# Seven Strassen products of a GeGLU up projection in another order: the product with the four-quarter weight sum moves from fourth to sixth place

## The chip, the cores and the metric

The kernel runs on 1 core of one Trainium2 chip. The metric is device time in microseconds (us) of one execution; each kernel's number is the median of several runs. The kernel before took 1378.93 us in the median of 3 runs (1378.06 to 1379.33).

## The reference, cut to what matters

The model is a two-layer encoder (512 tokens, width 1024, float32). Each layer ends in a GeGLU channel mixer, and the change lies in its up projection `hn @ w_up`, which has 2 x 2816 output columns: a gate half and a value half.

```python
def conv_geglu_ffn(hn, w_up, conv_w, conv_b, w_down):
    u = depthwise_conv_centered(hn @ w_up, conv_w, conv_b)
    gate, val = jnp.split(u, 2, axis=-1)
    return (jax.nn.gelu(gate, approximate=True) * val) @ w_down
...
for layer in range(DEPTH):
    ...
    f = conv_geglu_ffn(rms_norm(x, norm_ffn_pre[layer]), ffn_w_up[layer], ffn_conv_w[layer],
                       ffn_conv_b[layer], ffn_w_down[layer])
    x = x + rms_norm(f, norm_ffn_post[layer])
```

## The kernel before, in words

**Three-term products.** Every float32 factor is held as a high half and a low half (`hi + lo`). `split` (L104 on) makes them: a cast on ScalarE (L107) writes the high half, a subtraction on VectorE (L108) writes the low half. One product is then three matmuls (`mm3`): high by high (L116), low activation by high weight or its mirror (L117), and the third pairing (L118). In the up projection the weights are the stationary operand, so L116 and L118 need the high half of the weight (`whi`) and L117 needs its low half (`wlo`).

**The up projection.** The 22 column blocks `f` (128 gate and 128 value columns each) are walked in `ffn` (L500 on). Blocks 0 to 5, 12, 13, 20 and 21 are done plainly: two projections (gate and value) of 24 matmuls each, 512 tokens wide. The pairs that start at f = 6, 8, 10, 14, 16, 18 (`UP`, L391) go through `up_strassen`: seven products instead of eight, each of 24 matmuls 256 tokens wide, into PSUM tiles `mm` (banks `a`) and `pu` (banks `b` and `d`). So three Strassen pairs stand in a row, then two plain blocks, then three pairs, then two plain blocks, then the down projection. Both layers do the same.

**What one pair needs.** Four weight quarters of 128 x 1024 are loaded through SyncE's DMA queue: `q[11]` into a tile `wu`, `q[12]` and `q[22]` into `wst` (3 buffers, shared with all other weight loads), `q[21]` into `gain` (2 buffers). Seven weight blocks are multiplied: q11, q12+q22, q11+q12+q22, q11+q12+q21+q22, q11+q12, q21 and q22 in this order. The four additions are on VectorE (L451), 128 x 1024 each. Each block is split into one of 4 `whi` and one of 4 `wlo` buffers, so a split has to wait until the product four places earlier has read its buffers.

**What comes out.** Results are copied by ScalarE or added by VectorE into `G` and `V` (L487 to L495). Then `tail` does the convolution, the gelu and the gating product for the pair's two column blocks: per block 2 activations for the convolution (L511) and one gelu (L518) on ScalarE, 4 convolution steps (L512, L513) and one product into `H` (L520) on VectorE. In between, `E.chore` issues copies and accumulating copies of the down weights from GpSimd's queue (L274), each tied to a finished product.

**What sets the order.** The code is written with tiles; a scheduler puts the instructions of each engine into one fixed order by readiness and priority, and every engine then works its list strictly in that order. The weight preparation stands under a raised priority (L455), but only the order that the scheduler found counts at run time: an addition or a split can stand behind convolution steps that were ready earlier.

Of the kernel before, what the change touches and what calls it, by code (L numbers as in the profile page):

```python
# [8 lines left out]
F32 = mybir.dt.float32  # L9
# [8 lines left out]
P = 128  # L18
S = 512
NT = S // P  # L20
D = 1024
# [411 lines left out]
def up_strassen(E, pool, w_up, f, X, G, V):  # L433

    nc, tc = E.nc, E.tc
    low, high = slice(0, HW), slice(HW, S)

    def load(pool, name, s, h, tag=None):  # L440
        st = pool.tile([P, 1024], F32, name=name, tag=tag or name)
        nc.sync.dma_start(st.rearrange("p (f c) -> p f c", f=2),
                          w_up[s, f:f + 2, :, h * 512:h * 512 + 512].rearrange("f p c -> p f c"))
        return st

    def parts(st):
        hi, lo = E.whi.tile([P, 1024], R32, name="whi"), E.wlo.tile([P, 1024], R32, name="wlo")
        E.split(hi, lo, st)
        return hi, lo

    add = lambda o, x, y: nc.vector.tensor_tensor(o, x, y, op=ALU.add)  # L451
    q = {}

    def weights(i):
        with tc.high_priority(60):  # L455
            if i == 0:
                q[11] = load(pool, "wu", 0, 0, f"e{UP.index(f) % 2}")
                return parts(q[11])
            if i == 1:
                q[12], q[22] = load(E.wst, "wst", 1, 0), load(E.wst, "wst", 1, 1)  # L460
                add(q[11], q[11], q[12])
                add(q[12], q[12], q[22])
                return parts(q[12])
            if i == 2:
                q[0] = E.gain.tile([P, D], F32, name="gain")
                add(q[0], q[11], q[22])
                return parts(q[0])
            if i == 3:
                q[21] = load(E.gain, "gain", 0, 1)
                add(q[0], q[0], q[21])  # L470
                return parts(q[0])
            return parts(q[{4: 11, 5: 21, 6: 22}[i]])

    a = [E.mm.tile([P, S], F32, name="mm") for _ in range(2)]
    b, d = ([E.px.tile([P, S], F32, name="pu", tag="px") for _ in range(2)] for _ in range(2))
    order = ("A11", a), ("S3", b), ("S2", a), ("A22", b), ("R1", a), ("A12", d), ("S4", a)
    for i, (n, bank) in enumerate(order):
        hi, lo = weights(i)
        more = i in (2, 3, 4, 6)
        for j in range(2):  # L480
            for k in range(4):
                c = slice(j * 512 + k * P, j * 512 + k * P + P)
                E.mm3(bank[j][:, :HW], hi[:, c], lo[:, c], X[n][0][:, k], X[n][1][:, k], not more and k == 0, k == 3, more)
        if i == 4:
            t = E.tmp.tile([P, 2, HW], F32, name="w5", tag="tmp")
        for j in range(2):
            r = bank[j][:, :HW]  # L487
            if i in (3, 5):
                o = G[:, j, low if i == 3 else high]
                add(o, r, o)  # L490
            else:
                o = t[:, j] if i == 4 else {0: G[:, j, high], 1: V[:, j, low], 2: G[:, j, low], 6: V[:, j, high]}[i]
                nc.scalar.copy(o, r)
        if i == 4:
            add(V[:, :, low], t, V[:, :, low])  # L495
        if i in (1, 3, 5):
            E.chore()


def ffn(E, w_up, cw, w_down, ts, g_post_row, done, w1=None):  # L500
# [3 lines left out]
    with ExitStack() as ctx:  # L504
# [41 lines left out]
        for f in range(2, NF):  # L546
            if f in UP or f - 1 in UP:
                if f in UP:
                    G, V = (cp.tile([P, 2, S], F32, name=n, tag=t) for n, t in
                            ((("G", "k0"), ("V", "k1")) if UP.index(f) % 2 else (("G", "k2"), ("V", "k3"))))  # L550
                    up_strassen(E, hp, w_up, f, X, G, V)
                    for j in range(2):
                        tail(f + j, G[:, j], V[:, j], True)
                continue
            ps = []
            for s in range(2):
                behind = w1 and f == 2
                st = E.wload(w_up[s, f], E.mid if behind and s == 0 else None)
                w = E.wunit(None, st=st, behind=E.turned[3][1] if behind else None)
                ps.append(E.mm.tile([P, S], F32, name="mm"))  # L560
                E.proj_fm(ps[-1], w)
            tail(f, *ps)
            E.chore(2)
            if f < UP[0]:
                X = next(make)
            if f == NF - 2:
                big = hp.tile([P, 3, HK, HW], R32, name="big")
                for k in range(0, HK, 4):
                    c = slice(k, min(k + 4, HK))
                    E.split(big[:, 0, c], big[:, 1, c], H[:, c, HW:])  # L570
# [889 lines left out]
```

## Time and profile before

| | |
|---|---|
| median of 3 runs | 1378.93 us |
| the profiled execution's own time | 1380.18 us |
| its span on the core | 1378.4 us |
| mean granted TensorE clock | 0.998 |
| first three Strassen pairs, layer 1 (f = 6, 8, 10) | 342.77 to 405.70 us |
| second three Strassen pairs, layer 1 (f = 14, 16, 18) | 427.49 to 491.50 us |
| the same, layer 2 | 1096.02 to 1158.94 and 1180.73 to 1244.74 us |

The times of the profile are microseconds from the start of the span. A row of the timeline is: start, duration, engine, line, operation, what it writes and reads, size, count, and in brackets the idle time of the engine just before it with what ended that. Durations of neighbouring instructions of one engine overlap a little, so the pace of an engine is read from start to start.

### The profile page before, as it was taken

To read this page: it belongs to the slowest core of one execution; us is meant where nothing else is said; L and a number is where in the kernel's file an instruction comes from. 1 tells how busy PE (TensorE), PEld (TensorE's weight loads), DVE (VectorE), ACT (ScalarE), POOL (GpSimd) and SP (SyncE) were. 2 spreads that over 40 slices of the span, in tenths; PEclk is the share of its full clock that TensorE was granted. 3 is DMA by queue.
4 is the path that set the end of the run, shared out by engine and by line. 5 is a ranking of instruction groups with operands and counts; after the bars stand their busy time and mean duration, and the time that the engine had idled before them with its cause. 6 is when DMAs were issued, how large, how long until landed. Compare 5 with 4: busy or idle time off the path is not lost.

```text
span 1378.4 us, 20207 instructions
## 1 busy us (share of the span) xinstructions
PE 1342.7 (97%) x7640; PEld 1145.7 (83%) x7640; DVE 1125.3 (82%) x1578; ACT 838.5 (61%) x1399; POOL 108.3 (8%) x130
## 2 busy tenths in 40 slices
PE   7999999999999999999999999999999999999997
PEld 6877777898999988888678788787878899998886
DVE  7368888696888989797878776898789798898976
ACT  5356667444664666664878778477545466566663
POOL 1001110101001110010000110000010000110000
PEclk9999999999999999999999999999999999999999
DMA  8443232136669885564566455174445666977554
GB/s 296 143 138 102 87 98 92 49 123 229 212 207 213 190 226 194 189 206 127 144 176 193 123 185 166 60 200 119 133 131 169 202 229 189 221 187 202 191 188 145
DMA packets 75522, 229.94 MB, mean 167 GB/s; under 512 B 8352, under 2 KB 9120, under 8 KB 74912
## 3 DMA queue, kind: packets, MB, share of 16 engines
q1 hardware_dynamic: 60368, 167.30, 37.6%
q0 software_dynamic: 7168, 46.14, 13.6%
q10 hardware_dynamic: 7888, 15.21, 3.9%
q8 instruction: 60, 0.98, 0.3%
q14 instruction: 38, 0.31, 0.1%
HBM read 221.01 MB, written 51.64 MB: 198 GB/s over the span
## 4 chain that ended last, share of the span: by engine, by line
PE 77%; DVE 12%; ACT 4%; DMA 4%; issue 2%; POOL 1%; SPq 1%; DVEq 0%; POOLq 0%; ACTq 0%
PE mm L116 20%; PE mm L118 20%; PE mm L117 20%; DVE wlo L108 3%; PE pu L117 2%; PE pu L118 2%; PE pu L116 2%; DVE cv L512 1%; PE pi L1126 1%; PE st L1075 1%; DVE gain L451 1%; DMA pb<-pd 1%; DVE cv L513 1%; PE py L1146 1%; DMA wst<-in_c_fm 1%
## 5 line engine op out<-in xcount | busy, mean ns | idle before, releaser
L116 PE MATMUL mm<-xh,whi 128*128 128x512 f32 (+2 forms) x928 | 341.7, 368 | 0.6 <-ACT xh L107 0.2
L117 PE MATMUL mm<-xh,wlo 128*128 128x512 f32 (+2 forms) x928 | 340.6, 367 | 1.2 <-DVE wlo L108 1.2
L118 PE MATMUL mm<-xl,whi 128*128 128x512 f32 (+2 forms) x928 | 340.7, 368 | 0.5 <-DVE xl L108 0.5
L108 DVE TENSOR_TENSOR wlo<-wst,whi 128x1024 fp32r<-128x1024 f32 (+1 forms) x208 | 250.2, 1209 | 72.0 <-ACT whi L107 71.2
L107 ACT CAST whi<-wst 128x1024 fp32r<-128x1024 f32 (+1 forms) x208 | 214.0, 1033 | 116.1 <-PE mm L117 56.2
L116 PEld LDWEIGHTS mm<-xh,whi 128*128 128x128 f32 (+1 forms) x928 | 174.7, 188 | 30.8 <-issue 2.5
L117 PEld LDWEIGHTS mm<-xh,wlo 128*128 128x128 f32 (+1 forms) x928 | 174.7, 188 | 29.4 <-DVE wlo L108 1.6
L118 PEld LDWEIGHTS mm<-xl,whi 128*128 128x128 f32 (+1 forms) x928 | 174.4, 188 | 29.8 <-issue 1.3
L1105 ACT ACTIVATE pb<-pb,tok 128x128 f32<-128x128 f32 x256 | 80.9, 392 | 10.5 <-DMA pb<-pd 9.1
L116 PE MATMUL mm<-xc,whi 128*128 128x256 f32 x288 | 81.6, 284 | 1.8 <-ACT whi L107 1.8
L117 PE MATMUL mm<-xc,wlo 128*128 128x256 f32 x288 | 81.7, 284 | 1.5 <-DVE wlo L108 1.5
L118 PE MATMUL mm<-xc,whi 128*128 128x256 f32 x288 | 81.4, 283 | 0.0
L116 PE MATMUL mm<-whi,big 128*128 128x512 f32 x164 | 64.0, 390 | 0.0
L118 PE MATMUL mm<-wlo,big 128*128 128x512 f32 x164 | 63.8, 389 | 0.0
L117 PE MATMUL mm<-whi,big 128*128 128x512 f32 x164 | 63.8, 389 | 0.0
L511 ACT ACTIVATE cv<-mm,cwt 128x512 f32<-128x512 f32 x40 | 31.0, 776 | 53.0 <-PE mm L118 53.0
L117 PE MATMUL pu<-xh,wlo 128*128 128x256 f32 x192 | 54.8, 287 | 3.9 <-DVE wlo L108 3.6
L116 PEld LDWEIGHTS mm<-xc,whi 128*128 128x128 f32 x288 | 55.1, 192 | 2.6 <-ACT whi L107 2.6
L117 PEld LDWEIGHTS mm<-xc,wlo 128*128 128x128 f32 x288 | 55.3, 192 | 1.9 <-DVE wlo L108 1.9
L118 PEld LDWEIGHTS mm<-xc,whi 128*128 128x128 f32 x288 | 55.3, 192 | 0.0
L118 PE MATMUL pu<-xl,whi 128*128 128x256 f32 x192 | 54.0, 283 | 0.0
L116 PE MATMUL pu<-xh,whi 128*128 128x256 f32 x192 | 53.4, 285 | 0.2
(362 smaller groups left out, 3081.9 us busy)
## 6 DMA issues: line engine op xcount, KB each, us to landing
ts<-in_f_down POOLq DMA_DIRECT2D x48, 704.0 KB, 6.3
wst<-in_f_up SPq DMA_DIRECT2D x64, 512.0 KB
wst<-in_c_fm SPq DMA_DIRECT2D x40, 512.0 KB
wst<-ts SPq DMA_DIRECT2D x32, 512.0 KB
pb<-pd ACTq DMA_DIRECT2D x29, 512.0 KB
wst<-in_f_down SPq DMA_DIRECT2D x24, 512.0 KB
ts<-ts POOLq DMA_DIRECT2D x16, 704.0 KB, 7.8
wst<-in_ab_fm SPq DMA_DIRECT2D x20, 512.0 KB
```

Of the source, the lines that this page charges most:

```text
L107: first = self.nc.scalar.copy(hi, src)
L108: second = self.nc.vector.tensor_tensor(lo, src, hi.bitcast(F32), op=ALU.subtract)
L116: mm(out, lh, rh, start=first, stop=False)
L117: mm(out, ll, rh, start=False, stop=False)
L118: self.product = mm(out, lh, rl, start=False, stop=last)
L451: add = lambda o, x, y: nc.vector.tensor_tensor(o, x, y, op=ALU.add)
L511: nc.scalar.activation(o, ps, AF.Identity, scale=w(1), bias=w(3))
L512: nc.vector.scalar_tensor_tensor(o[:, 1:], ps[:, :S - 1], w(0), o[:, 1:], op0=ALU.mult, op1=ALU.add)
L513: nc.vector.scalar_tensor_tensor(o[:, :S - 1], ps[:, 1:], w(2), o[:, :S - 1], op0=ALU.mult, op1=ALU.add)
L1075: nc.tensor.matmul(ps, o["bt"][:, c], xs, start=True, stop=True)
L1105: nc.scalar.activation(pb[:, dr, c], pb[:, dr, c], AF.Identity, scale=1.0 - 2 * dr, bias=tok[:, 0, c, dr * H + h:dr * H + h + 1])
L1126: nc.tensor.matmul(pi[:, c - 1 + dr], o["st"][dr, i][:, q * P:(q + 1) * P], o["t"][1][:, c * C:(c + 1) * C], start=True, stop=True)
```

## The change

Inside each of the 12 Strassen pairs, the fourth and the sixth product trade places: the product of q21 (with A12, bank `d`) is now fourth, the product of the four-quarter sum (with A22, bank `b`) is sixth. The number of matmuls, splits, additions and loads stays the same. What changes with it:

- q11+q12 is written into a fresh `gain` tile instead of over `q[11]`.
- q11+q12+q22, for the third product, is written over `q[12]`, which the second product's split has read just before. Before it went into a fresh `gain` tile.
- The four-quarter sum is written over `q[11]`, which was split for the first product. Before it was written over the third product's sum, right after that one's split.
- `q[12]` keeps its `wst` buffer until the third product's split instead of the second's; `q[21]` is split directly, with no addition ahead of the fourth product.

```diff
             if i == 1:
                 q[12], q[22] = load(E.wst, "wst", 1, 0), load(E.wst, "wst", 1, 1)
-                add(q[11], q[11], q[12])
+                q[0] = E.gain.tile([P, D], F32, name="gain")
+                add(q[0], q[11], q[12])
                 add(q[12], q[12], q[22])
-                return parts(q[12])
             if i == 2:
-                q[0] = E.gain.tile([P, D], F32, name="gain")
-                add(q[0], q[11], q[22])
-                return parts(q[0])
+                add(q[12], q[0], q[22])
             if i == 3:
                 q[21] = load(E.gain, "gain", 0, 1)
-                add(q[0], q[0], q[21])
-                return parts(q[0])
-            return parts(q[{4: 11, 5: 21, 6: 22}[i]])
+            if i == 5:
+                add(q[11], q[12], q[21])
+            return parts(q[(11, 12, 12, 21, 0, 11, 22)[i]])
...
-    order = ("A11", a), ("S3", b), ("S2", a), ("A22", b), ("R1", a), ("A12", d), ("S4", a)
+    order = ("A11", a), ("S3", b), ("S2", a), ("A12", d), ("R1", a), ("A22", b), ("S4", a)
...
-        more = i in (2, 3, 4, 6)
+        more = i in (2, 4, 5, 6)
...
-                o = G[:, j, low if i == 3 else high]
+                o = G[:, j, low if i == 5 else high]
```

The scheduler then finds other orders. The first place is VectorE's list in the middle of the pair f = 8 of layer 1 (its tiles are `wu_3430`, `wst_3462`, `wst_3464`, `gain_3499` or `gain_3466`, and `gain_3531` for q21), while the convolution of the pair f = 6 is under way. Before:

```order
L451 TENSOR_TENSOR G_3166<-pu_3173,G_3166 128x256
L108 TENSOR_TENSOR wlo_3469<-wst_3462,whi_3468 128x1024
L512 SCALAR_TENSOR_TENSOR cv0_3402<-G_3166,cwt_2605,cv0_3402 128x511
L108 TENSOR_TENSOR wlo_3502<-gain_3499,whi_3501 128x1024
L513 SCALAR_TENSOR_TENSOR cv0_3402<-G_3166,cwt_2605,cv0_3402 128x511
L512 SCALAR_TENSOR_TENSOR cv1_3407<-V_3167,cwn_2607,cv1_3407 128x511
L512 SCALAR_TENSOR_TENSOR cv0_3412<-G_3166,cwt_2605,cv0_3412 128x511
L513 SCALAR_TENSOR_TENSOR cv1_3407<-V_3167,cwn_2607,cv1_3407 128x511
L513 SCALAR_TENSOR_TENSOR cv0_3412<-G_3166,cwt_2605,cv0_3412 128x511
L520 TENSOR_TENSOR H_2577<-cv0_3402,cv1_3407 128x512
L512 SCALAR_TENSOR_TENSOR cv1_3417<-V_3167,cwn_2607,cv1_3417 128x511
L451 TENSOR_TENSOR gain_3499<-gain_3499,gain_3531 128x1024
```

And now:

```order
L451 TENSOR_TENSOR wst_3462<-gain_3466,wst_3464 128x1024
L451 TENSOR_TENSOR G_3166<-pu_3171,G_3166 128x256
L509 SCALAR_TENSOR_TENSOR cv0_3402<-G_3166,cwt_2605,cv0_3402 128x511
L451 TENSOR_TENSOR wu_3430<-wst_3462,gain_3531 128x1024
L510 SCALAR_TENSOR_TENSOR cv0_3402<-G_3166,cwt_2605,cv0_3402 128x511
L509 SCALAR_TENSOR_TENSOR cv1_3407<-V_3167,cwn_2607,cv1_3407 128x511
L509 SCALAR_TENSOR_TENSOR cv0_3412<-G_3166,cwt_2605,cv0_3412 128x511
L510 SCALAR_TENSOR_TENSOR cv1_3407<-V_3167,cwn_2607,cv1_3407 128x511
L510 SCALAR_TENSOR_TENSOR cv0_3412<-G_3166,cwt_2605,cv0_3412 128x511
L517 TENSOR_TENSOR H_2577<-cv0_3402,cv1_3407 128x512
L108 TENSOR_TENSOR wlo_3502<-wst_3462,whi_3501 128x1024
L509 SCALAR_TENSOR_TENSOR cv1_3417<-V_3167,cwn_2607,cv1_3417 128x511
```

(L509, L510 and L517 are L512, L513 and L520 of before: the file is three lines shorter.) The split for the third product, `wlo_3502`, stood behind one convolution step and now stands behind six of them and a product into `H`. The four-quarter sum stood behind seven convolution steps and now stands behind one; its own split, `wlo_3598`, is the fifth row below the last one shown. The split for the fourth product was the third row below the last one shown; now it is the first, and reads q21.

The second place is SyncE's DMA queue, which works its list in order; the rows are the loads for the pairs f = 8 and f = 10 (`wst_3718` and `wst_3720` are q12 and q22 of f = 10). Before:

```order
L442 DMA wst_3464<-in_f0_up 128x2x512
L442 DMA wu_3686<-in_f0_up 128x2x512
L442 DMA wst_3718<-in_f0_up 128x2x512
L442 DMA gain_3531<-in_f0_up 128x2x512
L442 DMA wst_3720<-in_f0_up 128x2x512
```

And now:

```order
L442 DMA wst_3464<-in_f0_up 128x2x512
L442 DMA gain_3531<-in_f0_up 128x2x512
L442 DMA wu_3686<-in_f0_up 128x2x512
L442 DMA wst_3718<-in_f0_up 128x2x512
L442 DMA wst_3720<-in_f0_up 128x2x512
```

The load of q21 moved two places ahead. `wst_3720` still follows `wst_3718`, but it takes the buffer of `wst_3462`, which is now given back by the third product's split (`wlo_3502`) instead of the second's (`wlo_3469`).

The third place is TensorE's list at the start of the fourth product of the pair f = 8. Before:

```order
L118 MATMUL mm<-xc,whi 128x256
L116 MATMUL pu<-xh,whi 128x256 x2
L117 MATMUL pu<-xh,wlo 128x256
L118 MATMUL pu<-xl,whi 128x256
L116 MATMUL pu<-xh,whi 128x256
```

And now:

```order
L118 MATMUL mm<-xc,whi 128x256
L116 MATMUL pu<-xh,whi 128x256
L117 MATMUL pu<-xh,wlo 128x256
L118 MATMUL pu<-xl,whi 128x256
L116 MATMUL pu<-xh,whi 128x256
```

Two high-by-high matmuls stood ahead of the first one that reads the low half; now it is one, as everywhere else. Such a doubled first row now stands only at the third product of the pair f = 18, in both layers.

More of the change, by code (lines that the diff above doesn't have):

```diff
@@ L457, in weights @@
                 q[11] = load(pool, "wu", 0, 0, f"e{UP.index(f) % 2}")
-                return parts(q[11])
             if i == 1:
                 q[12], q[22] = load(E.wst, "wst", 1, 0), load(E.wst, "wst", 1, 1)
-                add(q[11], q[11], q[12])
+                q[0] = E.gain.tile([P, D], F32, name="gain")
+                add(q[0], q[11], q[12])
                 add(q[12], q[12], q[22])
-                return parts(q[12])
             if i == 2:
-                q[0] = E.gain.tile([P, D], F32, name="gain")
-                add(q[0], q[11], q[22])
-                return parts(q[0])
+                add(q[12], q[0], q[22])
             if i == 3:
                 q[21] = load(E.gain, "gain", 0, 1)
-                add(q[0], q[0], q[21])
-                return parts(q[0])
-            return parts(q[{4: 11, 5: 21, 6: 22}[i]])
+            if i == 5:
+                add(q[11], q[12], q[21])
+            return parts(q[(11, 12, 12, 21, 0, 11, 22)[i]])
     a = [E.mm.tile([P, S], F32, name="mm") for _ in range(2)]
     b, d = ([E.px.tile([P, S], F32, name="pu", tag="px") for _ in range(2)] for _ in range(2))
-    order = ("A11", a), ("S3", b), ("S2", a), ("A22", b), ("R1", a), ("A12", d), ("S4", a)
+    order = ("A11", a), ("S3", b), ("S2", a), ("A12", d), ("R1", a), ("A22", b), ("S4", a)
     for i, (n, bank) in enumerate(order):
         hi, lo = weights(i)
-        more = i in (2, 3, 4, 6)
+        more = i in (2, 4, 5, 6)
         for j in range(2):
```

## Prediction, made before the changed kernel ran

> **What bounds the kernel now.** I read the page's summary first, then the windows of the Strassen stretches, then TensorE's timeline inside them, then VectorE's, ScalarE's and the DMA queue's lists at the places where TensorE stops. Engine rows of the page are busy time, share of the span, instructions; the last row is the chain that ended last, by engine.
>
> ```profile
> span 1378.4 us, 20207 instructions
> PE 1342.7 (97%) x7640; PEld 1145.7 (83%) x7640; DVE 1125.3 (82%) x1578; ACT 838.5 (61%) x1399; POOL 108.3 (8%) x130
> PE 77%; DVE 12%; ACT 4%; DMA 4%; issue 2%; POOL 1%; SPq 1%; DVEq 0%; POOLq 0%; ACTq 0%
> ```
>
> TensorE sets the time, and 12% of the chain goes through VectorE: there TensorE is late because of it. The four stretches of three Strassen pairs in the windows view (length, then busy time of PE, PEld, DVE, ACT, POOL with counts, granted clock, DMA share, GB/s):
>
> ```profile
> 342.77:405.70 62.93, 61.51 (x506) 60.72 (x504) 53.95 (x66) 38.69 (x62) 5.82 (x11) 1.00 0.62 212
> 427.49:491.50 64.01, 61.75 (x505) 60.74 (x504) 56.93 (x70) 38.62 (x63) 9.53 (x11) 1.00 0.89 210
> 1096.02:1158.94 62.92, 61.49 (x505) 60.70 (x504) 53.96 (x66) 38.29 (x62) 5.82 (x11) 1.00 0.63 211
> 1180.73:1244.74 64.01, 61.74 (x505) 60.73 (x504) 58.90 (x72) 40.80 (x66) 9.54 (x11) 1.00 0.86 206
> ```
>
> The bounds are the first matmul of the first pair and the first one after the third. How long a pair takes without a stop is seen at f = 6, whose first matmul and whose successor's first are these:
>
> ```profile
> 342.77 0.28 PE L116 MATMUL mm<-xh,whi 128*128 128x256 f32 x1
> 362.93 0.28 PE L116 MATMUL mm<-xh,whi 128*128 128x256 f32 x1
> ```
>
> That is 20.16 us for 168 matmuls, 0.12 us each, 2.88 us a product. Three pairs need 60.48 us, so the stretches lose 62.93 - 60.48 = 2.45, 64.01 - 60.48 = 3.53, 2.44 and 3.53 us: **11.95 us** in all. The stops of layer 1 in TensorE's timeline:
>
> ```profile
> 371.56 0.40 PE L116 MATMUL pu<-xh,whi 128*128 128x256 f32 x2
> 372.87 0.39 PE L117 MATMUL pu<-xh,wlo 128*128 128x256 f32 x1 [0.91 <-DVE wlo L108]
> 393.98 0.38 PE L116 MATMUL mm<-xc,whi 128*128 128x256 f32 x1 [0.44 <-ACT whi L107]
> 457.58 0.38 PE L117 MATMUL pu<-xh,wlo 128*128 128x256 f32 x1 [0.91 <-DVE wlo L108]
> 475.86 0.39 PE L117 MATMUL mm<-xc,wlo 128*128 128x256 f32 x1 [0.75 <-DVE wlo L108]
> 479.80 0.38 PE L116 MATMUL mm<-xc,whi 128*128 128x256 f32 x1 [0.44 <-ACT whi L107]
> ```
>
> The first and third are the fourth product of f = 8 and f = 16, waiting for the low half of the four-quarter sum. The second and fifth are the fourth and fifth products of f = 10 and 18, where that sum, its cast and the casts queued behind it come late. The fourth is the third product of f = 18. So every stop but one hangs on the four-quarter sum being fourth. The chain at f = 8, on VectorE and ScalarE:
>
> ```profile
> 363.30 1.22 DVE L108 TENSOR_TENSOR wlo<-gain,whi 128x1024 fp32r<-128x1024 f32 x1
> 364.44 0.74 DVE L513 SCALAR_TENSOR_TENSOR cv<-G,cwt,cv 128x511 f32<-128x511 f32 x1
> 365.10 0.74 DVE L512 SCALAR_TENSOR_TENSOR cv<-V,cwn,cv 128x511 f32<-128x511 f32 x1
> 367.75 0.68 DVE L520 TENSOR_TENSOR H<-cv,cv 128x512 f32<-128x512 f32 x1
> 368.35 0.74 DVE L512 SCALAR_TENSOR_TENSOR cv<-V,cwn,cv 128x511 f32<-128x511 f32 x1
> 369.01 1.21 DVE L451 TENSOR_TENSOR gain<-gain 128x1024 f32<-128x1024 f32 x1
> 370.26 1.05 ACT L107 CAST whi<-gain 128x1024 fp32r<-128x1024 f32 x1 [1.00 <-DVE gain L451]
> 371.60 1.22 DVE L108 TENSOR_TENSOR wlo<-gain,whi 128x1024 fp32r<-128x1024 f32 x1
> ```
>
> The third product's split starts at 363.30, the addition over the same tile only at 369.01, behind six convolution steps and a product; its cast follows at 370.26, the low half is there at 372.82. TensorE wanted it 0.12 after 371.57, at 371.69. VectorE works without a gap here, but it is not short of time in the stretch: 53.95 us busy of 62.93. What was needed first simply stood last.
>
> **The change, part by part.** Splits, additions, matmuls and loads keep their number and shape, so no engine's sum changes. Paces, start to start, from the rows above: 1.14 us for a 128x1024 operation on VectorE, 0.66 for a convolution step, 0.60 for a product into H. Others, at the end of f = 6:
>
> ```profile
> 355.56 1.23 DVE L108 TENSOR_TENSOR wlo<-wu,whi 128x1024 fp32r<-128x1024 f32 x1 [0.65 <-ACT whi L107]
> 356.82 1.23 DVE L451 TENSOR_TENSOR wu<-wu,wst 128x1024 f32<-128x1024 f32 x1
> 359.70 0.41 DVE L451 TENSOR_TENSOR G<-pu,G 128x256 f32<-128x256 f32 x1
> 360.04 1.21 DVE L451 TENSOR_TENSOR gain<-wu,wst 128x1024 f32<-128x1024 f32 x1
> 357.37 0.37 ACT L493 COPY w<-mm 128x256 f32<-128x256 f32 x1 [1.07 <-PE mm L118]
> 359.87 1.05 ACT L107 CAST whi<-wst 128x1024 fp32r<-128x1024 f32 x1 [2.13 <-DVE wst L451]
> 360.82 0.81 ACT L511 ACTIVATE cv<-G,cwt 128x512 f32<-128x512 f32 x1
> ```
>
> An addition into G takes 0.34, a cast on ScalarE 1.05 from start to end.
>
> *First sums of a pair.* They no longer wait for the first product's split and stand before it in the new list, so the cast for the second product no longer waits 2.13 us for a sum: it can start after the copy of 357.37, at 357.63, and ends at 358.68.
>
> *The new order at f = 8*, from there by hand, with TensorE's block still at 362.93: second split 358.70; G 359.84; third product's sum 360.18; G 361.32; convolution 361.65; four-quarter sum 362.31; five convolution steps 363.45 to 366.75; H; third split at 367.36, its low half there at 368.58 (cast of that sum 361.42 to 362.47). TensorE wants it at 362.93 + 2 x 2.88 + 0.12 = 368.81: in time by 0.23. One convolution step later, 369.16, comes q21's split, there at 370.38 against 371.69: in time by 1.3. **The stop of 372.87 - 371.69 = 1.18 us goes.** What was moved behind the convolution steps, the third split, is what becomes late next, and it just fits. The sixth product's split is done at 373.9 against 377.45 needed.
>
> *At f = 10*, TensorE's block starts 20.16 later, 383.09. Its first split starts 375.67, when the fourth product of f = 8 has freed its buffer (374.45) and the cast of 1.05 is done. Then split 1.14, sum 1.14, V 0.60, sum 1.14, G 0.34, the second G waiting for the sixth product of f = 8 (380.35), the cast of the second product's sum to 380.85, split 1.14, convolution 0.66, sum 1.14, five steps 3.30, H 0.60: third split 387.71, low half there at 388.93. Wanted: 383.09 + 5.88 = 388.97. In time by 0.04. The kernel before has the same rows on VectorE between the fourth product's end and this split, and shows what such a margin is worth:
>
> ```profile
> 384.25 0.28 PE L116 MATMUL mm<-xh,whi 128*128 128x256 f32 x1
> 388.78 1.22 DVE L108 TENSOR_TENSOR wlo<-gain,whi 128x1024 fp32r<-128x1024 f32 x1
> ```
>
> There f = 10 started at 384.25, wanted this half at 390.13 and had it at 390.00; TensorE did not stop. The fourth, fifth and sixth products then have 0.8 us or more. *At f = 16* the order is that of f = 8; *at f = 18* the same working gives 471.18 for the third split against 465.36 + 5.76 + 0.24 = 471.36, since two high-by-high matmuls stand first there.
>
> *In-place sum right behind a split.* A 128x1024 operation that overwrites what the one before it has read starts 356.82 - 355.56 = 1.26 after it instead of 1.14; the new list puts a row between, so I take 0, at most 0.12 for each of 12.
>
> *Loads.* q22 of f = 10 takes a buffer given back by the third split (368.6) instead of the second (362.75 in the row below). A load can take 7 us to land when the queues are full: the one issued at 397.82 was cast at 404.81.
>
> ```profile
> 362.75 0.37 SPq L442 DMA_DIRECT2D wst<-in_f_up  x1
> 397.82 2.23 SPq L76 DMA_DIRECT2D wst<-in_f_up  x2
> 404.81 1.05 ACT L107 CAST whi<-wst 128x1024 fp32r<-128x1024 f32 x1 [3.35 <-DMA wst<-in_f_up]
> ```
>
> So it lands by 375.6; the addition that reads it starts at 378.55 in the working above. Cover 2.9 us, cost 0. Behind the third pairs TensorE reaches f = 20 and 21 about 6 us sooner, and loads may not follow. The first split for f = 21 was held up by its load before:
>
> ```profile
> 492.52 1.23 DVE L108 TENSOR_TENSOR wlo<-wst,whi 128x1024 fp32r<-128x1024 f32 x1 [2.58 <-ACT whi L107]
> ```
>
> Its half was there at 493.75 and wanted at 491.50 + 10.9 = 502.4 (half of the plain stretch of 427.49 - 405.70); 8.6 us in hand, 2.6 left after the 6. I take 0 here, with up to 2 us a layer as the upper end.
>
> *The sum.* 11.95 us of stops go; for the margins of 0.04 and 0.18 at f = 10 and 18, which are finer than such a working, I put 0.1 back at each in both layers, 0.4. The profiled execution took 1380.18 us (span 1378.4), 1.25 above the median, so 1380.18 - 11.55 = 1368.63 for such an execution and 1378.93 - 11.55 = **1367.4** for the median. The runs shown lie 0.1% apart; 0.2%, 2.8 us, is about what a measurement of this kernel can tell from no change.
>
> **The rivals.** *The third product takes the stop over.* Its split now stands behind the convolution. If one more 128x1024 operation's time (1.14) gets in front, through a late cast or load, it is late by 1.14 less the margin: 0.91 at f = 8 and 16, 1.10 at 10, 0.96 at 18, together 3.9 a layer and 7.8 in all: 1367.0 + 7.8 = 1374.8. For it: margins under 0.25 and a full VectorE. Against it: the margin of 0.13 at f = 10 before held.
>
> *Nothing to gain.* VectorE's work is the same, 7 splits and 4 additions a pair; if its sum sets the pace, stops only move: 1378.9. [...] Against it: VectorE has 9 us idle in the first stretch of 62.93 and 7 in the second of 64.01; and by the pair 355.56 and 356.82 a dependence does cost 0.12.
>
> *Slower: a late load heads VectorE's list.* The buffer of q12 is held one product's split longer, so q22 of f = 10 and 18 arrives about 5.8 us later. Its addition stands ahead of the splits, and nothing passes it. From 10 us of landing time on (368.6 to 378.55), each further us stops TensorE by one, four times in the run; past about 13 us the loss exceeds the 12 us gained. At 14 us: 1367 + 4 x 4 = 1383. For it: DMA shares of 0.89 and 0.86 in the second stretches. Against it: 7 us in the slowest landing quoted.
>
> **How the numbers follow.** The forecast (stops gone, under 2 us left over) gets 0.70, the third product's stop 0.18, nothing to gain 0.07, slower 0.05. The first two are both faster by over 0.2%: 0.88; same 0.07; slower 0.05. The low end is all stops gone, 1367.0, and a run as far below its median as the fastest shown (0.9): 1366.0. The high end takes in the 2 us a layer behind the pairs and the lower part of the first rival: 1372.0.
>
> **What would show it.** In the changed profile the pairs of layer 1 should start 20.16 us apart throughout, f = 12 start at 403.3 and f = 20 at 485.5; no wait of the fourth or fifth product for L107 or L108; a rest, if any, at the third product of f = 10 or 18. Wrong would be: waits of `mm` L117 at third products of over 0.5 us each, VectorE idle on an addition that waits for a load, or stretches of 60.5 us with the 6 us given back in the plain blocks or the down projection.

## The result, and the profile after

The changed kernel took 1381.45 us in the median of 22 runs (1376.79 to 1386.52); the kernel before, beside it, 1378.05 us (1376.31 to 1383.19, 22 runs). The ratio is 1.0022, with a 95% interval from 1.0013 to 1.0031: **slower by about 0.2%**, where 1367.4 us, 0.8% faster, had been forecast. The profiled execution took 1380.37 us, on a span of 1378.6.

The page of the changed kernel, TensorE's busy time and the chain that ended last:

```profile
PE 1340.7 (97%) x7640; PEld 1144.3 (83%) x7640; DVE 1123.0 (81%) x1578; ACT 835.3 (61%) x1399; POOL 110.2 (8%) x130
PE 71%; DVE 13%; DMA 6%; ACT 5%; issue 3%; POOL 0%; DVEq 0%; SPq 0%; POOLq 0%; ACTq 0%
```

VectorE has not left the chain (12% before, 13% now), and transfers stand in it with 6% instead of 4%. Where the time went is seen when the windows go on behind the pairs. Of the changed kernel, for each layer: first three pairs, second three pairs, the plain blocks f = 20 and 21, the first product of the down projection (length, busy time of PE, PEld, DVE, ACT, POOL, clock, DMA share, GB/s):

```profile
341.72:402.43 60.71, 60.71 (x505) 60.52 (x504) 55.05 (x68) 38.76 (x63) 5.82 (x11) 1.00 0.64 216
424.22:486.49 62.27, 60.98 (x505) 60.57 (x504) 58.62 (x73) 39.55 (x64) 9.51 (x11) 1.00 0.89 210
486.49:510.26 23.77, 22.10 (x98) 17.95 (x97) 13.79 (x18) 11.60 (x16) 1.76 (x2) 1.00 0.83 216
510.26:528.32 18.06, 15.77 (x67) 12.15 (x66) 16.30 (x19) 10.53 (x14) 0.00 (x0) 1.00 0.44 143
1096.76:1157.48 60.72, 60.72 (x506) 60.52 (x505) 55.04 (x68) 38.45 (x62) 5.82 (x11) 1.00 0.62 212
1179.26:1241.59 62.33, 60.98 (x506) 60.57 (x504) 58.88 (x73) 39.55 (x64) 9.54 (x11) 1.00 0.88 204
1241.59:1263.81 22.22, 22.08 (x98) 17.95 (x97) 18.40 (x23) 12.41 (x17) 1.78 (x2) 1.00 0.80 209
1263.81:1278.84 15.03, 15.03 (x68) 12.31 (x66) 11.91 (x14) 9.94 (x12) 0.00 (x0) 1.00 0.57 193
```

The last two stretches of layer 1 in the kernel before (layer 2 has the same lengths):

```profile
491.50:513.29 21.79, 21.79 (x98) 18.04 (x97) 19.57 (x24) 14.74 (x21) 1.76 (x2) 1.00 0.85 220
513.29:528.25 14.96, 14.96 (x67) 12.39 (x66) 13.86 (x13) 9.26 (x11) 0.00 (x0) 1.00 0.48 152
```

The stops that the change was to remove are gone: the first stretches went from 62.93 and 62.92 to 60.71 and 60.72, where 60.48 is three pairs without a stop. The second stretches lost only 1.74 and 1.68 of their 3.53. Behind them 23.77 - 21.79 = 1.98 us came back in the plain blocks of layer 1, 3.10 in the first down product, and 0.43 and 0.07 in layer 2. TensorE's timeline names the new stops of layer 1 (f = 14, f = 16, f = 21, the first and the second down product), and in the last row the one at layer 2's second down product:

```profile
430.97 0.39 PE L116 MATMUL mm<-xc,whi 128*128 128x256 f32 x1 [0.84 <-ACT G L490]
451.96 0.39 PE L117 MATMUL mm<-xc,wlo 128*128 128x256 f32 x1 [0.45 <-DVE wlo L108]
499.46 0.50 PE L117 MATMUL mm<-xh,wlo 128*128 128x512 f32 x1 [1.67 <-DVE wlo L108]
513.61 0.47 PE L116 MATMUL mm<-whi,big 128*128 128x512 f32 x1 [1.82 <-DVE cv L510]
531.53 0.50 PE L118 MATMUL mm<-wlo,axh 128*128 128x512 f32 x1 [2.60 <-DVE wlo L108]
1282.07 0.50 PE L118 MATMUL mm<-wlo,axh 128*128 128x512 f32 x1 [2.62 <-DVE wlo L108]
```

From start to start each is about 0.16 longer than its bracket, so the second down product gives back 2.75 in layer 1 and 2.78 in layer 2. The account of what the change touches: -2.22 - 1.74 - 2.20 - 1.68 = -7.84 in the pairs, +1.98 + 3.10 + 0.43 + 0.07 = +5.58 behind them, +5.53 in the second down products: **+3.27 us**. The medians lie 3.4 apart; that a sum from one execution of each kernel comes so near to them is partly luck. The spans of the two profiled executions lie only 0.2 apart, because this one reached f = 6 1.05 us sooner and made up 2.1 more between the layers; the stretch from the second down product to layer 2's f = 6, with its stops, took from 564.3 to 571.2 us in the profiled executions of this study.

### The profile page after: what moved, and what is told of

Same layout as the page of the kernel before. It is cut to its first block, busy times and chain, and to the rows that moved or that the text cites. A ratio compares the mean times of both kernels' runs of the same rounds, so it can differ in the third digit from the quotient of the medians.

```text
span 1378.6 us, 20187 instructions
## 1 busy us (share of the span) xinstructions
PE 1340.7 (97%) x7640; PEld 1144.3 (83%) x7640; DVE 1123.0 (81%) x1578; ACT 835.3 (61%) x1399; POOL 110.2 (8%) x130
## 4 chain that ended last, share of the span: by engine, by line
PE 71%; DVE 13%; DMA 6%; ACT 5%; issue 3%; POOL 0%; DVEq 0%; SPq 0%; POOLq 0%; ACTq 0%
PE mm L118 19%; PE mm L116 19%; PE mm L117 19%; DVE wlo L108 4%; DMA wst<-in_f_up 3%; DVE cv L509 1%; PE pi L1123 1%; DMA pb<-pd 1%; DVE cv L510 1%; PE st L1072 1%; PE pu L118 1%; PE pu L117 1%; PE pu L116 1%; ACT whi L107 1%; PE py L1143 1%
## 5 line engine op out<-in xcount | busy, mean ns | idle before, releaser
L108 DVE TENSOR_TENSOR wlo<-wst,whi 128x1024 fp32r<-128x1024 f32 (+1 forms) x220 | 264.4, 1209 | 71.2 <-ACT whi L107 70.5
L107 ACT CAST whi<-wst 128x1024 fp32r<-128x1024 f32 (+1 forms) x220 | 225.8, 1033 | 128.3 <-PE mm L117 47.3
L515 ACT ACTIVATE cv<-cv 128x512 f32<-128x512 f32 x44 | 27.7, 631 | 48.2 <-DVE cv L510 48.1
```

Source lines behind the costliest of these rows:

```text
L107: first = self.nc.scalar.copy(hi, src)
L108: second = self.nc.vector.tensor_tensor(lo, src, hi.bitcast(F32), op=ALU.subtract)
L515: nc.scalar.activation(g, g, AF.Gelu_apprx_tanh)
```

## What stands ahead of the new stops

ScalarE's and VectorE's timelines of the changed kernel, first at f = 14, then from f = 20 into the down projection:

```profile
409.83 1.23 DVE L451 TENSOR_TENSOR gain<-wu,wst 128x1024 f32<-128x1024 f32 x1 [2.56 <-DMA wst<-in_f_up]
428.41 0.63 ACT L515 ACTIVATE cv<-cv 128x512 f32<-128x512 f32 x1 [2.72 <-DVE cv L510]
...
491.75 1.05 ACT L107 CAST whi<-wst 128x1024 fp32r<-128x1024 f32 x1 [6.17 <-DMA wst<-in_f_up]
493.95 0.75 DVE L509 SCALAR_TENSOR_TENSOR cv<-V,cwn,cv 128x511 f32<-128x511 f32 x1 [5.37 <-ACT cv L508]
498.18 1.22 DVE L108 TENSOR_TENSOR wlo<-wst,whi 128x1024 fp32r<-128x1024 f32 x1
508.70 1.05 ACT L107 CAST whi<-wst 128x1024 fp32r<-128x1024 f32 x1 [6.88 <-DMA wst<-in_f_down]
509.78 1.23 DVE L108 TENSOR_TENSOR wlo<-wst,whi 128x1024 fp32r<-128x1024 f32 x1 [4.39 <-ACT whi L107]
```

The cast for f = 21's first block waits 6.17 us for its load. Behind it on ScalarE stand the convolution activations of f = 18 and 19; VectorE's next convolution steps need these, so VectorE sits idle for 5.37 us; and the new list has put that block's split behind five convolution steps and a product into H. The split starts at 498.18, TensorE stops until 499.46. The same happens with a down weight at 508.70: its load was issued at 499.46, right behind the late split, which ended at 499.40; in the kernel before, the load behind that split was issued at 493.77. So the engine that a row names (`<-DVE wlo L108`) is not the cause: two lists further back stands a load.

That load was issued at 481.68 and cast at 491.75, 10.1 us later. In the DMA view of the changed kernel from 476 to 492 us (queue, packets, MB, share of the 16 engines' time), the copies on GpSimd's software queue and the loads on SP's queue fill the engines to 104% (a packet that starts in the window is counted with its whole time):

```profile
q0 software_dynamic: 439, 1.67, 52.3%
q1 hardware_dynamic: 817, 3.01, 51.6%
```

The copies took as much of the engines' time as the loads, with 439 packets against 817. In what order the engines served the two queues is shown by no run.

Why do the loads crowd together here? One of them comes late, and what holds it is a buffer. The new four-quarter sum reads `q[12]` once more, so `q[12]` keeps its `wst` buffer until that sum, and not only until the third product's split as the list of what the change does has it, wherever the sum is the later of the two. At f = 18 it is. VectorE's and SyncE's rows in the kernel before, the second product's split and the load of f = 20's second block, which takes that buffer:

```profile
469.54 1.22 DVE L108 TENSOR_TENSOR wlo<-wst,whi 128x1024 fp32r<-128x1024 f32 x1
470.79 0.34 SPq L76 DMA_DIRECT2D wst<-in_f_up  x1
```

And in the changed kernel, where the four-quarter sum stands in the split's place:

```profile
476.96 1.22 DVE L451 TENSOR_TENSOR wu<-wst,gain 128x1024 f32<-128x1024 f32 x1
478.20 0.33 SPq L76 DMA_DIRECT2D wst<-in_f_up  x1
```

Each load starts right behind the end of the row above it. Before, it was issued 20.7 us ahead of TensorE's first matmul of f = 20, now 8.3 us ahead, and f = 21's load follows 3.5 us behind it. (At f = 10 it is the same: f = 12's second load was issued at 384.98 before and at 393.40 now.)

Five theories were put to the test. Theory A: the transfer queues set the pace here; TensorE comes 5 us sooner, loads and copies do not, and what was gained is waited for. Its rivals: VectorE's new list orders cost by themselves (B); q12's buffer, held until the third split, delays loads (C); what the new list puts ahead of the loads on SP's queue costs (D), or ahead on VectorE at f = 14 (E).

## Experiments

| run | us, median | runs | ratio to before | 95% interval |
|---|---|---|---|---|
| before without copies | 1380.35 | 11 | 1.0012 | 1.0003 to 1.0020 |
| changed without copies | 1366.52 | 4 | 0.9914 | 0.9901 to 0.9927 |
| order alone | 1379.68 | 11 | 1.0007 | 0.9998 to 1.0015 |
| buffers alone | 1376.17 | 12 | 0.9988 | 0.9975 to 1.0000 |
| changed, copies earlier | 1389.84 | 6 | 1.0072 | 1.0056 to 1.0088 |
| before, copies earlier | 1379.17 | 12 | 1.0004 | 0.9994 to 1.0013 |
| change in 6, 8, 10 only | 1374.99 | 12 | 0.9979 | 0.9967 to 0.9990 |
| change in 14, 16, 18 only | 1382.58 | 12 | 1.0028 | 1.0017 to 1.0040 |
| changed, norm rows late | 1373.40 | 5 | 0.9950 | 0.9934 to 0.9965 |
| change in all but 14 | 1380.20 | 11 | 1.0009 | 0.9997 to 1.0020 |
| change in all but 14 and 18 | 1373.13 | 8 | 0.9964 | 0.9952 to 0.9977 |
| changed, no copies from f = 12 on | 1370.11 | 5 | 0.9936 | 0.9924 to 0.9948 |
| before, norm rows late | 1377.89 | 11 | 1.0003 | 0.9994 to 1.0012 |
| all but 14 and 18, rows late | 1375.22 | 12 | 0.9976 | 0.9963 to 0.9989 |
| changed, norm rows late, again | 1370.57 | 6 | 0.9951 | 0.9932 to 0.9969 |
| all but 14 and 18, again | 1373.24 | 5 | 0.9956 | 0.9944 to 0.9969 |

**Without the copies.** The edit is the same in both kernels:

```diff
-        E.chores = sums(E, ffns[0][2], ts[0])
+        E.chores = []
...
-    seq = ((w, 0), a), ((ts, 1), bb), ((ts, 2), a), ((ts, 3), bb), ((ts, 0), a), ((w, 2), d), ((w, 3), a)
+    seq = ((w, 0), a), ((w, 1), bb), ((w, 2), a), ((w, 3), bb), ((w, 0), a), ((w, 2), d), ((w, 3), a)
```

> The kernel before, without the 32 copies and accumulating copies on the GpSimd queue that prepare the sums of down-projection weights (704 KB each); the down projection reads plain weight quarters of the same size instead. Theory A (the transfer queues set the pace behind the pairs): before has only a few waits for loads, so it gains little, 0 to 4 us: 1374 to 1378. Theory B (VectorE's list orders cause the loss, not loads): the same, 1374 to 1378. This is the base of the next run.

> The changed kernel with the same copies left out, to be held against the kernel before without them. Theory A: the stops that the change removed now show, and nothing returns at f = 13, 14, 20, 21 and in the down projection: 8 to 12 us under the kernel before without copies, so about 1364 to 1368. Theory B: the loss stays, 0 to 4 us above the kernel before without copies.

Both then leave out the preparation of the down weights' sums. The kernel before gained nothing from it. The changed kernel fell to 1366.52 us, 13.8 below the kernel before without copies. Up to the down projection the two changed kernels have the same lists on SyncE's queue; only the copies are missing. The second stretch of layer 1, the plain blocks, and the cast and split for f = 21 in that run:

```profile
424.18:484.65 60.47, 60.47 (x506) 60.47 (x504) 55.64 (x69) 39.47 (x64) 0.00 (x0) 1.00 0.35 113
484.65:506.44 21.79, 21.79 (x99) 18.03 (x97) 20.15 (x25) 14.10 (x21) 0.00 (x0) 1.00 0.41 133
```

```profile
483.94 1.05 ACT L107 CAST whi<-wst 128x1024 fp32r<-128x1024 f32 x1 [0.99 <-DMA wst<-in_f_up]
490.38 1.22 DVE L108 TENSOR_TENSOR wlo<-wst,whi 128x1024 fp32r<-128x1024 f32 x1
```

No stop is left in the second three pairs. The load for f = 21, issued at 479.85, is cast 4.1 us later instead of 10.1, and the split, still behind the convolution steps, is in time. Theory B falls: where transfers have room (DMA shares of 0.35 and 0.41 here), the new lists cost nothing by themselves. (Here too the load of f = 20's second block is issued only 8.3 us ahead of f = 20.)

**Without the copies from f = 12 on.**

```diff
-        if i in (1, 3, 5):
+        if i in (1, 3, 5) and f < 12:
             E.chore()
...
-            E.chore(2)
+            if f < 12:
+                E.chore(2)
```

> The changed kernel without the copies from f = 12 on (15 of 32 left out in each layer, so that the down projection's sums are incomplete). Theory A (it is the copies beside the second three pairs that make loads late): 1366 to 1370, as without any copies. Rival (the copies beside the first pairs matter as much): 1373 to 1378.

It came to 1370.11, at the top of theory A's range. By the medians, 11.3 of the 14.9 us that the changed kernel gains without any copies belong to those behind f = 12. The stop at f = 14 stayed (1.04 us from start to start): the load that it hangs on is issued at about 400 us, beside the copies of f = 10.

**Order alone, buffers alone.** The first has the new products with the sums where they lay before, the second the new sums with the products in the old order (the accumulation flags and the halves of G follow the products):

```diff
-                q[0] = E.gain.tile([P, D], F32, name="gain")
-                add(q[0], q[11], q[12])
+                add(q[11], q[11], q[12])
                 add(q[12], q[12], q[22])
             if i == 2:
-                add(q[12], q[0], q[22])
+                q[0] = E.gain.tile([P, D], F32, name="gain")
+                add(q[0], q[11], q[22])
...
-                add(q[11], q[12], q[21])
-            return parts(q[(11, 12, 12, 21, 0, 11, 22)[i]])
+                add(q[0], q[0], q[21])
+            return parts(q[(11, 12, 0, 21, 11, 0, 22)[i]])
```

```diff
                 q[21] = load(E.gain, "gain", 0, 1)
-            if i == 5:
                 add(q[11], q[12], q[21])
-            return parts(q[(11, 12, 12, 21, 0, 11, 22)[i]])
+            return parts(q[(11, 12, 12, 11, 0, 21, 22)[i]])
...
-    order = ("A11", a), ("S3", b), ("S2", a), ("A12", d), ("R1", a), ("A22", b), ("S4", a)
+    order = ("A11", a), ("S3", b), ("S2", a), ("A22", b), ("R1", a), ("A12", d), ("S4", a)
```

> Only the order of products is changed (fourth q21, sixth the sum of four quarters); the sums lie in the buffers of before, so the weight buffer of q12 comes free with the second split as before. Theory A (queues full, whatever the buffer): about as the changed kernel, 1378 to 1382. Theory C (the buffer held until the third split delays the loads): the gain that was forecast, 1367 to 1371.

> Only the sums' buffers are changed (first sum in a new tile, three-quarter sum over q12, four-quarter sum over q11); the products keep the order of before, the sum of four quarters fourth. Theory A: the stops at the fourth product mostly stay, and so does the time, 1377 to 1380. Theory C: the held buffer costs without the gain of the order, 1382 to 1390.

The times of both went against theory C: the order alone gained nothing, though q12's buffer comes free early; the buffers alone were a little faster than before, if at all (the interval ends at 1.0000), and not slower. But the times do not settle it. With the order alone f = 20's second load is issued at 467.27, and nothing comes back at f = 20 and 21; instead q21, whose load stands behind that one in SyncE's list (issued at 467.66, in the changed kernel at 458.79) and which is now needed fourth, is late at f = 18:

```profile
474.15 1.04 ACT L107 CAST whi<-gain 128x1024 fp32r<-128x1024 f32 x1 [2.76 <-DMA gain<-in_f_up]
475.25 0.58 PE L116 MATMUL pu<-xh,whi 128*128 128x256 f32 x1 [3.79 <-ACT whi L107]
```

That is another place and the same kind of wait, and it hides what the early buffer is worth. Over all runs of this study the traces bear theory C out for this one load, as a part of the cause. In every profiled execution with the change at f = 18 the load is issued 8.1 to 8.3 us ahead of f = 20, and only among these the plain blocks lose time; where it was issued 13.8 us ahead (buffers alone) or 20.7 and more (the products or the sums of f = 18 as before), they took 21.79 us in both layers each time. The late load alone is not enough: without the copies, without those behind f = 12, and with the copies issued earlier, nothing was lost there either, and with the rows late (below) it was lost in one layer of four. No run moves this load and nothing else.

**Copies earlier.** Three behind the early plain blocks, four in each of the first pairs, one behind f = 12 and 13, two in the last pairs, in the changed kernel and in the one before:

```diff
-            E.chore(2)
+            E.chore(3 if f < 6 else 1)
...
         if i in (1, 3, 5):
-            E.chore()
+            E.chore(2 if i == 3 and f < 12 else 0 if i == 3 and f > 12 else 1)
```

> The changed kernel with the same 32 copies on the GpSimd queue issued earlier: three instead of two behind each plain block before f = 6, four instead of three in each of the pairs 6, 8, 10, one instead of two behind f = 12 and 13, two instead of three in 14, 16, 18, so that none is left behind f = 18. Theory A (the loads land late because copies crowd the queues from 402 us on): the stops behind f = 12 shrink, most of the gain of the run without copies comes back, 1367 to 1373. Rival (the copies cost the same wherever they lie, since all loads of the up projection share the queues with them): 1376 to 1381.

> The kernel before with the copies issued earlier in the same way. Its stops hang on the four-quarter sum and not on loads, so by theory A little moves: 1376 to 1380. If the copies were a cost by themselves, it would gain as much as the changed kernel does with them.

My remedy was wrong: 1389.84, 17 us above the top of what I had expected and 9 above the rival's. Behind f = 18 it did what it was meant to do: the plain blocks took 21.79 us in both layers. But the first and the second three pairs of layer 1 took 66.4 and 66.5 us. The windows from 382 to 424 us and a cast behind them show the copies doing their damage sooner (DMA share 0.93, against 0.52 from 382 to 402 in the changed kernel):

```profile
382.00:402.00 20.00, 17.82 (x136) 17.62 (x135) 15.87 (x22) 12.35 (x20) 2.05 (x3) 0.91 0.93 202
402.00:424.00 22.00, 22.00 (x129) 19.54 (x128) 11.92 (x15) 8.64 (x13) 3.12 (x4) 1.00 0.93 237
```

```profile
417.38 1.05 ACT L107 CAST whi<-wst 128x1024 fp32r<-128x1024 f32 x1 [10.31 <-DMA wst<-in_f_up]
```

What counted here is not that copies lie late, but that they lie beside loads that are due. The kernel before took the same move without a loss in the median; in its profiled execution the first three pairs of layer 1 took 65.9 us instead of 62.9.

**Half of the pairs.** The new scheme for some `f`, the old code for the others; the first run has `new = f < 12`, the second `new = f > 12`:

```diff
+    new = f < 12
...
+                if new:
+                    q[0] = E.gain.tile([P, D], F32, name="gain")
+                add(q[0 if new else 11], q[11], q[12])
...
+            return parts(q[((11, 12, 12, 21, 0, 11, 22) if new else (11, 12, 0, 0, 11, 21, 22))[i]])
```

> The change in the pairs f = 6, 8, 10 only; 14, 16 and 18 as before. Theory A: the 2.45 us a layer of the first three pairs go, TensorE comes earlier to f = 12 to 14, and the loads there give it back: 1377 to 1381. Rival (the loss comes from the new lists of the second three pairs): 1373 to 1375.

> The change in the pairs f = 14, 16, 18 only; 6, 8 and 10 as before. Theory A: 3.5 us a layer of stops go in the pairs, and part comes back at f = 20 and 21 and in the down projection, whose loads cannot come sooner: 1373 to 1379. Rival (the new lists of these pairs are what costs): 1380 to 1384.

Both came out on the rivals' side of my numbers. In the first three pairs the change holds what it gains: 60.71 us there, 1374.99 in all. In the second three it removes every stop and more than loses it behind them; second pairs, plain blocks and first down product of layer 1:

```profile
426.50:486.98 60.48, 60.48 (x506) 60.47 (x505) 56.00 (x70) 38.75 (x63) 9.52 (x11) 1.00 0.90 214
486.98:510.47 23.49, 22.08 (x99) 17.95 (x97) 14.39 (x19) 12.29 (x17) 1.76 (x2) 1.00 0.82 213
510.47:527.77 17.30, 15.73 (x68) 12.16 (x66) 15.53 (x18) 9.95 (x12) 0.00 (x0) 1.00 0.48 157
```

So theory A needs a place, not only a share: the end of the second three pairs, where the load of f = 20 waits for q12's buffer.

**The norm rows late.** SyncE's queue in the changed kernel at that place, and then with the two rows of norm gains tied behind f = 21's last product:

```profile
475.38 0.34 SPq L291 DMA_DIRECT2D wx<-in_f_down  x1
476.47 0.34 SPq L101 DMA_DIRECT2D gain<-in_norms  x1
478.20 0.33 SPq L76 DMA_DIRECT2D wst<-in_f_up  x1
478.62 0.38 SPq L101 DMA_DIRECT2D gain<-in_norms  x1
481.68 1.47 SPq L76 DMA_DIRECT2D wst<-in_f_up  x2
```

```profile
475.47 0.34 SPq L293 DMA_DIRECT2D wx<-in_f_down  x1
478.33 0.34 SPq L76 DMA_DIRECT2D wst<-in_f_up  x1
481.77 0.33 SPq L76 DMA_DIRECT2D wst<-in_f_up  x1
...
509.59 0.42 SPq L101 DMA_DIRECT2D gain<-in_norms  x1
```

```diff
-    def bcast(self, row):
+    def bcast(self, row, behind=None):
...
-        self.nc.sync.dma_start(g, row.partition_broadcast(P))
+        m = self.nc.sync.dma_start(g, row.partition_broadcast(P))
+        if behind:
+            self.together([m], [behind])
...
-        g_post = E.bcast(g_post_row)
+        g_post = E.bcast(g_post_row, E.product)
```

> The changed kernel, with the loads of the two rows of norm gains (layer 1; one in layer 2) held until f = 21's last product, so that they no longer stand ahead of the weight loads of f = 20 and 21 on SP's queue. Theory D (these rows, put ahead by the new list, delay the loads of f = 20, 21 and the first down weights): the stops of 1.83, 1.98 and part of 2.75 us of layer 1 go, 1375 to 1378. Theory A alone (the copies fill the queues, whatever stands ahead): 1379 to 1383.

> The kernel before with the two rows of norm gains held until f = 21's last product, as in the changed kernel with late rows. Theory D (the rows cost only where TensorE comes so early that the loads of f = 21 and of the down weights are short): before has 8 us in hand there, so nothing, 1377 to 1380. Rival (late rows gain by themselves, whatever the change): 1371 to 1374.

> The changed kernel with late rows once more, since its five times lay from 1369.5 to 1378.9: if the gain holds, a ratio to the kernel before of 0.993 to 0.998; if it was an accident of few runs, 0.999 to 1.003.

The weight loads are issued at the same moments as in the changed kernel, so nothing was waiting behind the rows in SyncE's list. But the 512 KB of each row no longer move beside those loads: from 476 to 492 us SP's queue moved 2.46 MB instead of 3.01, while the engines stayed as full (1.02 against 1.04). Of the repeated run's profile (the edit makes line numbers 2 higher):

```profile
488.79 1.05 ACT L109 CAST whi<-wst 128x1024 fp32r<-128x1024 f32 x1 [4.11 <-DMA wst<-in_f_up]
495.23 1.21 DVE L110 TENSOR_TENSOR wlo<-wst,whi 128x1024 fp32r<-128x1024 f32 x1
```

```profile
486.59:508.38 21.79, 21.79 (x99) 18.02 (x97) 18.02 (x23) 13.93 (x19) 1.76 (x2) 1.00 0.79 207
508.38:523.34 14.96, 14.96 (x68) 12.39 (x66) 13.19 (x13) 9.85 (x13) 0.00 (x0) 1.00 0.71 219
```

The load for f = 21 takes 7.0 us from issue to cast instead of 10.1, the split comes 2.95 us sooner, and the plain blocks and the first down product have no stop. Two sets of runs gave 0.9950 and 0.9951; the kernel before with late rows gave 1.0003, so the rows cost only where the change has taken the slack away. Theory D holds in so far as the rows' transfers cost, as a part of A. That the new list puts them ahead is not the reason: they stood ahead of f = 21's load in the kernel before as well (480.22 and 482.49, the load at 483.63), and f = 20's second load comes behind one of them because its buffer is held. The remedy is not stable: 11 runs lie between 1369.5 and 1379.1, and the first execution profiled, 1378.92, still lost 1.29 us in layer 2's plain blocks and 2.78 in its second down product.

**All but 14; all but 14 and 18.** The edit is the one above with `new = f != 14` and `new = f not in (14, 18)`.

> The change in all pairs but f = 14, which keeps the order and buffers of before. Theory E (at f = 14 the first sum stands at the head of VectorE's list with a load that is late, and holds the convolution and the copies behind it): the stops of 1.00 and 1.47 us at its third product go and so does what hangs on them, 1376 to 1379. Rival: TensorE then only comes sooner to f = 21 and the down projection and waits there: 1380 to 1383.

> The change in the pairs 6, 8, 10 and 16; 14 and 18 as before. In its lists the load for f = 20 is issued ahead of the norm rows again, and at f = 14 the load of q21 no longer stands between those of the other quarters. Theories D and E: the stops of f = 8, 10 and 16 go (2.45 + 1.1 a layer) and nothing returns: 1371 to 1374. Theory A alone: what goes returns behind f = 18, 1375 to 1379.

> The change in the pairs 6, 8, 10 and 16 and the rows late. If the two remedies are for the same loss, nothing is added to the version with 14 and 18 as before: 1372 to 1375. If the rows still cost there, 1369 to 1371.

> The change in the pairs 6, 8, 10 and 16 once more, beside the changed kernel with late rows on one chip: 0.995 to 0.998 as before if it holds.

With only f = 14 as before, its stop went and one of 1.69 us appeared at f = 16's third product; the time stayed at 1380.20, the rival's number, and theory E falls. With 18 as before too, q12's buffer comes free with the second split and f = 20's load is issued ahead of `wx` and the rows again, and 1373.13 and 1373.24 were measured, below both kernels. The plain blocks lose nothing in either profile, as expected; but the second three pairs took 64.72 and 63.84 us in layer 1, where f = 16 now stops at its third product, and 62.91 and 63.25 in layer 2, so the gain is in the main that of the first pairs. Late rows add nothing to it (1375.22): the two remedies mend the same loss.

## Why the prediction was wrong

*Stops of 11.95 us, hanging on the four-quarter sum being fourth:* right. Without the copies the changed kernel took 13.8 us less than the kernel before without them. The rival by which VectorE's sum sets the pace is refuted, since the number of its operations is the same in both; what decided here was their place in the list. The part of the 13.8 above 11.95 is no gain of the change: in that run the kernel before took 65.53 us for its second three pairs in both layers, instead of 64.01, at a mean granted clock of 0.97 instead of 1.00 (last section).

*f = 8 and 16, f = 10 and 18, margins of 0.23, 0.04 and 0.18:* right at f = 8, f = 10 and 18. f = 10 shows 0.14 us at 388.05, its third product, and nothing else; 0.1 had been put back there. f = 16, with 0.23 in hand by the working, lost 0.61 at its third product. Why is not shown: without a stop at f = 14 (all but 14) it lost 1.69.

*In-place sum, 0 to 0.12 each:* not separable; the first stretches exceed 60.48 by 0.23 in all.

*Loads of f = 10, cover 2.9 us:* right; no wait there.

**Loads behind the third pairs, "8.6 us in hand, 2.6 left after the 6. I take 0 here, with up to 2 us a layer as the upper end": this step failed.** Measured were 1.98 + 3.10 + 2.75 = 7.83 us in layer 1 and 0.43 + 0.07 + 2.78 = 3.28 in layer 2, and another 1.8 a layer at f = 14 and 16, where I had looked for no load at all. The working took from the kernel before that the half for f = 21 is there at 493.75, and moved only TensorE. Three things were wrong in it. The load did not come sooner with TensorE: in the kernel before it was issued at 483.63 and cast at 491.43, 7.8 us later; now f = 20's second load, issued at 470.79 before, waits for q12's buffer until the four-quarter sum is done and falls in among the rows and `wx` (478.20), the copies come in a shorter time (the three of f = 18 are issued within 11.5 us, 472.66 to 484.18, instead of 13.9, 475.29 to 489.20), and f = 21's load, issued 2 us sooner, took 10.1 us to its cast at 491.75. The prediction had seen that the buffer is held longer, but ended the hold at the third split and followed it to the next pair's q22 alone, not to f = 20. The split no longer followed its cast: the new list had put convolution steps between them, and those waited for activations behind the same cast, so the half came at 499.40. And the two late casts did not cost one product each, they stopped both lists: 5.37 and 4.39 us of idle VectorE, whose backlog reached into the down projection.

The slower rival named the right kind of event, a load made late by q12's buffer that then heads a list, at the wrong place (q22 of f = 10 and 18). "7 us in the slowest landing quoted" was no bound: that row came from a kernel whose TensorE left the queues more time, and the same kernel had one of 7.8. Of what was to show the forecast wrong, two came: VectorE idle on an addition that waits for a load (409.83), and time given back in the plain blocks and the down projection, though the pairs took more than 60.5 us.

What stays open: how the lateness divides between the late load of f = 20, the copies and the rows at each place. Leaving copies out changes all that is behind them, and the runs with late rows still differ by up to 9 us from one to the next.

## What to carry to other kernels

When a stop goes, walk the next loads through the *new* list: which buffer each takes and which instruction reads that buffer last, date of issue, landing under the load that the engines carry then, what stands between the landing and TensorE, and what stands behind the waiting instruction. A margin read from a kernel that was late is partly made of that lateness. Where the transfer engines were busy for 0.8 to 0.9 of the time, moving two transfers that were not yet due out of the way of those that were was worth 8 to 11 us here, and moving copies to another place without such a walk cost 8.

## What the hardware showed that I had not expected

A stop cost more than its length here. Change in 14, 16, 18 only, and the changed kernel, both after a stop of 2.75 us at the second down product (windows; the column ahead of the DMA share is the clock granted):

```profile
531.00:534.00 3.00, 3.00 (x7) 2.42 (x8) 3.00 (x4) 0.00 (x0) 0.00 (x0) 0.50 0.66 203
```

```profile
531.40:534.00 2.60, 2.47 (x11) 2.05 (x12) 2.60 (x4) 0.00 (x0) 0.00 (x0) 1.00 0.51 153
```

One went on at half clock for about 3 us, the other at full clock, after the same stop. Why the same stop cost one kernel its clock and the other not is shown by no run. After the stop of 3.95 us at f = 18 with the order alone the clock was 0.51 from 475.2 to 478.2 us (the first matmul behind it, at 475.25, took 0.58 us, where the one behind the stop at 430.97 in the changed kernel took 0.39), and after stops of 1.14, 0.61 and 0.44 us close together at f = 18 in the kernel before without copies it was 0.51 from 480 to 483. That is part of why the kernel before gained nothing without its copies: its second three pairs took 1.52 us longer in each layer, with stops that add up to as much as before.
